# Max unpooling: the first load of the indices, issued as four transfers of every fourth partition instead of one

## The chip, the core and the metric

The kernel runs on one core of a Trainium2 chip. The metric is the device time of one execution in microseconds (us); lower is better. Most executions of one kernel lie within 0.3% of each other. In the profile the engines are VectorE (DVE), ScalarE (ACT), GpSimd (POOL) and SyncE (SP); a "q" after the name means the engine's own queue of waits and issues. Beside them, 16 DMA engines move data between the chip's memory and SBUF, the on-chip memory of 128 partitions.

## The reference

```python
x: (16, 64, 32, 32) float32;  indices: same shape, values 0 to 3;  kernel_size = 2
output = zeros((16, 64, 64, 64), float32)
output[b, c, 2*i + idx // 2, 2*j + idx % 2] = x[b, c, i, j]    # idx = indices[b, c, i, j]
```

Each input element goes to one of four places of a 2x2 block, the other three stay zero.

## The kernel before

The 1,024 images lie on 128 partitions, eight on each. The indices are 64-bit in memory, so eight images of them are 64 KiB for each partition, those of x 32 KiB, and the result 128 KiB. VectorE computes `(idx == p) * x` for each of the four places. Three loads are issued ahead of everything: three images of the indices, all of x, the other five images of the indices. Four stores, of two images each, follow as the images are done.

```python
FIRST = 3
cut = FIRST * 2 * N                         # N = 1024; 32-bit words, two for an index
program.first(nc.sync.dma_start(out=idx_t[:, :cut], in_=idx_v[:, :cut]).then_inc(idx_in[0], 16))
program.first(nc.sync.dma_start(out=x_t, in_=x_v).then_inc(x_in, 16))
program.first(nc.sync.dma_start(out=idx_t[:, cut:], in_=idx_v[:, cut:]).then_inc(idx_in[1], 16))

nc.vector.wait_ge(x_in, 16).then_inc(x_in, -16)
for t in range(T):                          # 8 images
    if t in (0, FIRST):
        half = int(t == FIRST)
        nc.vector.wait_ge(idx_in[half], 16).then_inc(idx_in[half], -16)
    ...                                     # cut: four scalar_tensor_tensor for one or two images
for g in range(NG):                         # 4 stores
    nc.sync.wait_ge(made, g + 1)
    nc.sync.dma_start(out=out_v[g], in_=out_t[g])
```

Of the kernel before, what the change touches and what calls it, by code (L numbers as in the profile page):

```python
# [1 line left out]

# [4 lines left out]

P = 128
F32 = mybir.dt.float32
I32 = mybir.dt.int32  # L10


class Program:




    def __init__(self, nc):
        self.nc = nc
        self.block = nc.main_func.blocks[0]  # L20
        self.kernel_block = nc.cur_bb.bb.name

    def __enter__(self):
        ins = self.block.instructions
        self.branches = [i for i in ins if "Branch" in type(i).__name__]
        n = len(ins) - len(self.branches)
        assert all("Branch" in type(ins[k]).__name__ for k in range(n, len(ins)))
        del ins[n:]
        self.nc.switch_bb(self.block.name, parent=None)
        self.symbolic = self.nc._always_lower_symbolic_ap  # L30
        self.nc._always_lower_symbolic_ap = False
        return self

    def first(self, made):
        ins = self.block.instructions
        assert ins[len(ins) - 1].name == made.ins.name
        moved = ins.pop()
        at = next(
            k
            for k, i in enumerate(ins)  # L40
            if i.engine == moved.engine and isinstance(i, mybir.InstDrain)
        )
        ins.insert(at, moved)

    def last(self, made):


        def move(nc):
            ins = self.block.instructions
            at = next(k for k, i in enumerate(ins) if i.name == made.ins.name)  # L50
            nc.main_func.blocks[-1].instructions.append(ins.pop(at))

        self.nc.at_finalize(move)

    def __exit__(self, kind, *_):
        self.nc._always_lower_symbolic_ap = self.symbolic
        if kind is None:
            for b in self.branches:
                self.block.instructions.append(b)
            self.nc.switch_bb(self.kernel_block, parent=None)  # L60


@with_exitstack
def kernel(
    ctx: ExitStack,
    tc: tile.TileContext,
    x: bass.AP,
    indices: bass.AP,
    kernel_size: bass.AP,
    out: bass.AP,  # L70
):
    nc = tc.nc
    assert kernel_size == 2

    B, C, H, W = x.shape
    n_img = B * C
    T = n_img // P
    assert T * P == n_img and C % T == 0

    G = 2  # L80
    NG = T // G
    FIRST = 3
    N = H * W
    x_v = x.rearrange("b (ch t) h w -> (b ch) (t h w)", t=T)
    idx_v = indices.rearrange("b (ch t) h w -> (b ch) (t h w)", t=T).bitcast(I32)
    out_v = out.rearrange("b (ch g t) oh ow -> g (b ch) (t oh ow)", g=NG, t=G)

    x_t = nc.alloc_sbuf_tensor("x_t", [P, T * N], F32).ap()
    idx_t = nc.alloc_sbuf_tensor("idx_t", [P, T * 2 * N], I32).ap()
    out_t = [  # L90
        nc.alloc_sbuf_tensor(f"out_t{g}", [P, G * 4 * N], F32).ap()
        for g in range(NG - 1)
    ]
    out_t.append(out_t[0])

    x_in = nc.alloc_semaphore("x_in")
    idx_in = [nc.alloc_semaphore(f"idx_in{g}") for g in range(2)]
    made = nc.alloc_semaphore("made")
    stored_0 = nc.alloc_semaphore("stored_0")
    stored = nc.alloc_semaphore("stored")  # L100

    x_c = x_t.rearrange("p (t i j) -> p t i j", t=T, j=W)
    idx_c = idx_t.rearrange("p (t i j two) -> p t i j two", t=T, j=W, two=2)[
        :, :, :, :, 0
    ]
    cut = FIRST * 2 * N

    with Program(nc) as program:
        program.first(
            nc.sync.dma_start(out=idx_t[:, :cut], in_=idx_v[:, :cut]).then_inc(  # L110
                idx_in[0], 16
            )
        )
        program.first(nc.sync.dma_start(out=x_t, in_=x_v).then_inc(x_in, 16))
        program.first(
            nc.sync.dma_start(out=idx_t[:, cut:], in_=idx_v[:, cut:]).then_inc(
                idx_in[1], 16
            )
        )

        nc.vector.wait_ge(x_in, 16).then_inc(x_in, -16)
        for t in range(T):
            g, k = t // G, t % G
            if t in (0, FIRST):
                half = int(t == FIRST)
                nc.vector.wait_ge(idx_in[half], 16).then_inc(idx_in[half], -16)  # L126

            if k == 1 and t != FIRST:
                continue
            n = 1 if k == 1 or t + 1 == FIRST else 2  # L130
            if g == NG - 1:
                nc.vector.wait_ge(stored_0, 16).then_inc(stored_0, -16)
            o_c = out_t[g].rearrange(
                "p (m i two j wo) -> p m i two j wo", m=G, two=2, wo=2, j=W
            )
            for pidx in range(4):
                op = nc.vector.scalar_tensor_tensor(  # L137
                    out=o_c[:, k : k + n, :, pidx // 2, :, pidx % 2],
                    in0=idx_c[:, t : t + n],
                    scalar=pidx,  # L140
                    in1=x_c[:, t : t + n],
                    op0=mybir.AluOpType.is_equal,
                    op1=mybir.AluOpType.mult,
                )
            if k + n == G:
                op.then_inc(made, 1)

        for g in range(NG):
            nc.sync.wait_ge(made, g + 1)
            nc.sync.dma_start(out=out_v[g], in_=out_t[g]).then_inc(  # L150
                stored if g else stored_0, 16
            )
        nc.sync.sem_inc(made, -NG)
        program.last(
            nc.sync.wait_ge(stored, 16 * (NG - 1)).then_inc(stored, -16 * (NG - 1))
        )


# [1 line left out]
_INS = ['x', 'indices', 'kernel_size']  # L160
_OUTS = [((16, 64, 64, 64), 'float32')]

_NUMBERS = {'kernel_size': 2}


# [26 lines left out]
```

## Time and profile before

| what | value |
|---|---|
| time, median | 71.49 us (71.4 to 71.7, 6 runs) |
| bytes | 12.58 MB read, 16.78 MB written |
| VectorE busy | 35.6 us |
| DMA engines busy | 97.4% of the span |

The span in the profile leaves out some 1.3 us of the device time. One thing has to be said ahead: the profile of before was taken on an execution of 71.79 us, 0.3 over the median. That becomes important when two profiles are compared.

The issues that open the program, and the start of VectorE, from the timeline (start, duration, engine, line, operation, names, count):

```profile
0.00 0.38 SPq L110 DMA_DIRECT2D idx_t<-in_indices_dram  x1
0.43 0.42 SPq L114 DMA_DIRECT2D x_t<-in_x_dram  x1
0.90 0.43 SPq L116 DMA_DIRECT2D idx_t<-in_indices_dram  x1
...
19.67 35.60 DVE L137 SCALAR_TENSOR_TENSOR out_t<-idx_t,x_t 128x2048 f32<-128x2048 int32 x20 [19.67 <-DVEq L126]
```

SyncE needs 0.38 to 0.43 us to issue a load and is done with all three at 1.33 us. The packet records in the trace, one for each row of each transfer, say when data began to move: at 1.00 us, 0.62 after the end of the first issue. The rest of the profile is read in the prediction.

### The profile page before, as it was taken

The numbers are of one execution on the slowest core, as the hardware profiler recorded it, in microseconds if no ns is written. First come the engines' busy times: TensorE is split into PE (matmuls) and PEld (weight loads), VectorE is DVE, ScalarE is ACT, GpSimd is POOL, SyncE is SP. The second block draws the span as 40 slices with busy tenths as digits, with TensorE's granted clock in tenths as the row PEclk, the third lists the DMA queues.
The fourth block names the chain that finished last, engine by engine and source line by source line (L and its number), as shares of the span: only waits on it lengthen the run. The fifth ranks groups of instructions, "written<-read, shape, count | busy, mean of one in ns | idle before, by whom it ended". The sixth has DMA issues, their size and how long they took to land.

```text
span 70.5 us, 72 instructions
## 1 busy us (share of the span) xinstructions
DVE 35.6 (51%) x20; POOL 0.2 (0%) x4
## 2 busy tenths in 40 slices
DVE  0000000000089999999999999999999300000000
POOL 1000000000000000000000000000000000000000
DMA  8799997979988999869898999989898989999891
GB/s 223 307 432 418 423 558 316 558 335 558 409 372 372 488 581 418 372 298 539 353 539 353 484 409 409 465 353 502 353 539 353 539 353 484 409 391 484 372 484 56
DMA packets 1008, 29.36 MB, mean 417 GB/s; under 512 B 112, under 2 KB 112, under 8 KB 112
## 3 DMA queue, kind: packets, MB, share of 16 engines
q1 hardware_dynamic: 1008, 29.36, 97.4%
HBM read 12.58 MB, written 16.78 MB: 417 GB/s over the span
## 4 chain that ended last, share of the span: by engine, by line
DVE 46%; DVEq 4%; issue 1%
DVE out_t L137 46%; DVEq L187 4%
## 5 line engine op out<-in xcount | busy, mean ns | idle before, releaser
L137 DVE SCALAR_TENSOR_TENSOR out_t<-idx_t,x_t 128x2048 f32<-128x2048 int32 (+1 forms) x20 | 35.6, 1860 | 19.7 <-DVEq L126 19.7
L173 POOL MEMSET const-bfloat16-1.0<- 128x1 bf16 x1 | 0.1, 103 | 0.0
L173 POOL MEMSET const-uint8-127<- 128x1 uint8 x1 | 0.1, 103 | 0.0
L173 POOL MEMSET const-float32-1.0<- 128x1 f32 x1 | 0.1, 100 | 0.0
L173 POOL MEMSET const-float32-0.0<- 128x1 f32 x1 | 0.1, 99 | 0.2 <-issue 0.2
## 6 DMA issues: line engine op xcount, KB each, us to landing
out_dram<-out_t SPq DMA_DIRECT2D x4, 4096.0 KB, 13.8
idx_t<-in_indices_dram SPq DMA_DIRECT2D x1, 5120.0 KB, 30.8
x_t<-in_x_dram SPq DMA_DIRECT2D x1, 4096.0 KB, 19.0
idx_t<-in_indices_dram SPq DMA_DIRECT2D x1, 3072.0 KB, 9.7
```

Of the source, the lines that this page charges most:

```text
L137: op = nc.vector.scalar_tensor_tensor(out=o_c[:, k : k + n, :, pidx // 2, :, pidx % 2], in0=idx_c[:, t : t + n], scalar=pidx, in1=x_c[:, t ...
L173: nc = _bacc.Bacc("TRN2", target_bir_lowering=False, num_devices=1)
L187: with _tile.TileContext(nc) as tc:
```

## The change

The first load becomes four transfers. Transfer o takes partitions o, o+4, ..., o+124, that is 32 rows spread over the whole of SBUF; such a transfer of every n-th partition is called a comb below. Bytes, row length and order of the three loads stay. The likely intent is to start with smaller transfers without giving up the reach over all partitions.

```diff
+    COMB = 4
 ...
-        program.first(
-            nc.sync.dma_start(out=idx_t[:, :cut], in_=idx_v[:, :cut]).then_inc(
-                idx_in[0], 16
+        for o in range(COMB):
+            rows = slice(o, None, COMB)
+            program.first(
+                nc.sync.dma_start(out=idx_t[rows, :cut], in_=idx_v[rows, :cut]).then_inc(
+                    idx_in[0], 16
+                )
             )
-        )
 ...
-                nc.vector.wait_ge(idx_in[half], 16).then_inc(idx_in[half], -16)
+                n_in = 16 if half else 16 * COMB
+                nc.vector.wait_ge(idx_in[half], n_in).then_inc(idx_in[half], -n_in)
```

## The prediction

> **What bounds the kernel now.** I read the busy tenths of the page first, then the DMA queue, then the stretches of the span one by one, then the chain that ended last. The page:
>
> ```profile
> span 70.5 us, 72 instructions
> ...
> DVE  0000000000089999999999999999999300000000
> ...
> DMA  8799997979988999869898999989898989999891
> ...
> q1 hardware_dynamic: 1008, 29.36, 97.4%
> HBM read 12.58 MB, written 16.78 MB: 417 GB/s over the span
> ```
>
> The reader is to see that VectorE works only in the middle (35.6 us of 70.5) and stops 15 us before the end, while the DMA row is full from the first slice to the last but one. The 16 DMA engines move packets for 97.4% of the span. The same in stretches that I cut at the borders of the transfers:
>
> ```profile
> 0.00:1.00 1.00, 0.00 (x0) 0.20 (x4) 1.00 0.00 0
> 1.00:2.00 1.00, 0.00 (x0) 0.00 (x0) 1.00 1.45 393
> 2.00:3.00 1.00, 0.00 (x0) 0.00 (x0) 1.00 0.89 369
> 3.00:5.00 2.00, 0.00 (x0) 0.00 (x0) 1.00 0.94 406
> 5.00:8.70 3.70, 0.00 (x0) 0.00 (x0) 1.00 0.99 425
> 8.70:18.40 9.70, 0.00 (x0) 0.00 (x0) 1.00 1.00 432
> 18.40:30.60 12.20, 10.93 (x6) 0.00 (x0) 1.00 1.00 432
> ```
>
> The last two columns are the DMA share and GB/s. Nothing moves in the first microsecond; the first load then climbs to 425 GB/s; from 8.7 us on it is flat at 432. (Shares above 1 only mean that a packet is counted whole at its start.)
>
> The packet records under this view give the arithmetic. There are 128 rows in each of seven transfers, 896 data packets, and 112 semaphore writes of 4 bytes. A row of 24,576 B takes 0.912 us, one of 32,768 B 1.213, one of 40,960 B 1.514; the next row on the same engine starts about 4 ns before the old one ends, so they cost 0.908, 1.210 and 1.511. Each engine has 8 rows of each transfer: 8 x (0.908 + 1.210 + 1.511 + 4 x 1.210) = 67.7 us. First packets start at 1.00 to 1.48 us and the last packet ends at 70.1. So no engine has more than about 2.4 us that is not steady transfer. On the engine that ends last I find them all: start 1.14, its first row 1.87 instead of 0.91 (0.96), one row of the second index load 0.25 too long. The first row is slow on all 16 engines (1.15 to 1.87), the second clearly so on three only, by at most 0.25, and no later row of this load.
>
> That VectorE does not matter is in the issues and the chain:
>
> ```profile
> SPq L150 <- DVE out_t L137: 52.5, 4, 26.9
> SPq L155 <- SPq L155: 14.1, 1, 14.1
> ```
>
> These are SyncE's waits. Stores are issued as images are done, the last at 55.3 us, but the third store's last bytes leave at 60.4 us, so the fourth waits in the rings for 4.3 us at least and up to 5 us: VectorE could be that much later at no cost. The page's chain (46% VectorE) does not see this queue; I don't follow it.
>
> [...] 32 rows still give 16 engines, two rows each, and 64 increments are the right count for four transfers. The trace agrees for 128 rows: eight rows for each of 16 engines, 16 semaphore writes for each transfer.
>
> [...] 24,576 B in 0.908 us is 27.1 GB/s on each engine, all 16 at once, without a row at half speed after the start. [...]
>
> [...] the three loads here queue behind each other without a gap.
>
> **The change, part by part.** Removed: one issue of 3,072 KB. Added: four of 768 KB with the same rows, row length and total bytes. An engine's share is still 8 rows of 24,576 B, 7.3 us.
>
> Issues: the three load issues took 0.38, 0.42 and 0.43 us of SyncE, one after the other from 0.00, 0.43 and 0.90. Three more delay the issue of x by 3 x 0.45 = 1.4 us, to about 1.8, and that of the second index load to about 2.3. The rings run dry only if an engine finishes two rows (1.8 us) before the next issue arrives (0.45 us later), so this is hidden. x is wanted at 8.8 us.
>
> Semaphore writes: three more for each engine. In the trace such a write takes 9 ns and the next row starts 6 ns after its start: 3 x 6 = 0.02 us. Nothing.
>
> Waits: VectorE waits for x (19.6 us) before it looks at the first index load; 64 increments instead of 16 cost it nothing.
>
> Start: the first packets still wait for the first issue, whose length does not seem to come from the number of rows (a store with rows of another size takes 0.34). If fewer rows meant sooner packets I could gain at most the spread of first starts, 0.48 us.
>
> Which rows an engine gets: this is the one part that can move the time. The transfer has partitions o, o+4, ..., o+124. Two ways to deal 32 rows to 16 engines:
> (a) [...] sum +0.0 to +0.1 us.
> (b) in consecutive pairs: [...] a row takes 1.82 instead of 0.91, eight rows 14.5 instead of 7.3: +7.3 us. [...] All later transfers and VectorE shift along; since the DMA stays the bound, all of it reaches the end.
>
> **The rivals.** First, the same (rival a): [...] It makes 71.5. Second, a gain at the start: shorter transfers, or other rows read at the same moment, could take away part of the slow first rows (0.25 to 0.96 us too long) or of the 0.8 us between the first and the last engine at the end. Against it: the first row of each engine is still its first, and byte counts are unchanged. All of it together is under 1.43 us, the 2% of 71.51; it makes 71.0. Third, issue starvation: every issue would have to cost over 1.8 us; measured 0.43. It makes nothing.
>
> **Range and chances.** The time has two humps: 71.2 to 71.7 (a), and about 75 to 78.8 (b), that is 71.5 plus 3.5 to 7.3. I hold (b) somewhat the likelier[...]. I choose a number in (b), with the discount for slipping: 71.5 + 5.0 = 76.5. The range has to span both. Slower 0.54, same 0.44, faster 0.02.
>
> **What would show it.** In (b): rows of the first load at 1.3 to 1.8 us throughout, the first 3.1 MB landing at about 13 to 16 us instead of 9.7 after issue, about 200 to 280 GB/s in the stretch 3 to 8.7 us, VectorE starting at about 25 instead of 19.67, and from x on everything as before (432 GB/s), only later. In (a): rows of 0.91 again from the third on, VectorE at 19.6 to 19.8, SyncE's six load issues over by 2.8 us. I would be wrong altogether if the rows after x changed their 1.21 us, if the DMA row showed a hole between the small transfers, or if the last store came to wait for VectorE.

## The result

The changed kernel takes 71.91 us (71.85 to 72.26, 6 runs) against 71.49: the same within 2%, and 0.69% slower (95% interval 0.41% to 0.96%). Here and below a ratio is the mean time of one kernel's fast runs over that of the other's of the same rounds, so it is not quite the ratio of the medians. The predicted 76.5 us did not come; the time fell into the lower of the prediction's two humps, a little above its upper edge.

The page of the changed kernel:

```profile
span 70.5 us, 75 instructions
...
DMA  7699989696988889966969696989979696969894
...
q1 hardware_dynamic: 1056, 29.36, 97.4%
HBM read 12.58 MB, written 16.78 MB: 416 GB/s over the span
```

There are 48 more packets, which are the semaphore writes of three more transfers (3 x 16). The DMA row is still full, and the first digit went from 8 to 7. The span is 70.5 us, the same as before. A reader who compares only these two pages would find no loss at all. But the first page is of an execution that took longer than usual (71.79 us; the six timed ones took 71.4 to 71.7). A second profile of the unchanged kernel, on one of 71.56 us, opens with

```profile
span 70.2 us, 72 instructions
```

so the pages agree with the loss that the timed runs show, and I compare with both profiles below.

The stretches of the changed kernel (the last two columns are DMA share and GB/s):

```profile
1.00:2.00 1.00, 0.00 (x0) 0.00 (x0) 1.00 1.47 369
2.00:3.00 1.00, 0.00 (x0) 0.00 (x0) 1.00 0.41 172
3.00:5.00 2.00, 0.00 (x0) 0.00 (x0) 1.00 1.13 479
5.00:8.70 3.70, 0.00 (x0) 0.00 (x0) 1.00 1.01 432
8.70:18.40 9.70, 0.00 (x0) 0.00 (x0) 1.00 1.01 437
```

A packet is counted whole at its start. With all 16 engines nearly in step this makes the second and third stretch look like a hole followed by a burst. It is none: first rows that began at 1.33 to 2.03 us last until about 3, and no engine pauses between two rows. From 5 us on the rate is 432 to 437 GB/s (before: 425 to 432). After the first rows nothing ran at half speed.

What did move is at the very beginning:

```profile
0.00 0.55 SPq L113 DMA_DIRECT2D idx_t<-in_indices_dram  x1
...
2.52 0.60 SPq L117 DMA_DIRECT2D x_t<-in_x_dram  x1
3.17 0.45 SPq L119 DMA_DIRECT2D idx_t<-in_indices_dram  x1
...
19.92 35.60 DVE L141 SCALAR_TENSOR_TENSOR out_t<-idx_t,x_t 128x2048 f32<-128x2048 int32 x20 [19.92 <-DVEq L130]
```

The first issue takes 0.55 us instead of 0.38, and the four together 2.48. VectorE starts at 19.92 us instead of 19.67, and does the same 35.6 us of work. A stepped issue is not the only thing that takes longer: the issue of x, whole as before, takes 0.60 us behind the four instead of 0.42; why is open.

The packet records do not name the DMA engine. But a packet starts some 4 ns before the one ahead of it on the same engine ends (6 ns after the start of a semaphore write), so they can be chained into 16 sequences. Each of the 16 has eight rows of the first load in both kernels; in the changed one they come in twos between semaphore writes in 14 of the 16, two rows of each of the four transfers. In these:

| packet records | before, 71.79 us | before, second profile, 71.56 us | changed, 71.85 us |
|---|---|---|---|
| very first packet starts (us) | 1.00 | 1.01 | 1.33 |
| first packet, mean of 16 engines | 1.16 | 1.23 | 1.52 |
| rows of the first load: median, and excess over it for each engine in all | 0.912, 0.57 | 0.912, 0.53 | 0.912, 0.66 |
| rows of x, mean start | 13.25 | 13.27 | 13.70 |
| last semaphore write: first, mean, last engine | 69.30, 69.57, 70.11 | 69.34, 69.55, 69.86 | 69.80, 69.96, 70.13 |

The excess is what the slow rows at the start, the ramp, cost beyond eight steady rows. The mean engine ends 0.39 to 0.42 us later, and it was already 0.43 to 0.45 late in the rows of x. So the whole loss is made in the first load. Against the second profile its terms are 0.29 (first packets), 0.13 (longer first rows) and 0.02 (semaphore writes), together 0.43. The last column also shows why the pages looked equal: the slowest engine in the first profile of before was 0.5 us behind the mean, in the changed kernel only 0.2.

### The profile page after: what moved, and what is told of

Read it like the earlier page. It is cut to its first block, busy times and chain, and to the rows that moved or that the text cites. A ratio compares the mean times of both kernels' runs of the same rounds, so it can differ in the third digit from the quotient of the medians.

```text
span 70.5 us, 75 instructions
## 1 busy us (share of the span) xinstructions
DVE 35.6 (50%) x20; POOL 0.2 (0%) x4
## 4 chain that ended last, share of the span: by engine, by line
DVE 46%; DVEq 4%; issue 1%
DVE out_t L141 46%; DVEq L191 4%
## 5 line engine op out<-in xcount | busy, mean ns | idle before, releaser
L141 DVE SCALAR_TENSOR_TENSOR out_t<-idx_t,x_t 128x2048 f32<-128x2048 int32 (+1 forms) x20 | 35.6, 1860 | 19.9 <-DVEq L130 19.9
```

The source lines that it names most:

```text
L141: op = nc.vector.scalar_tensor_tensor(out=o_c[:, k : k + n, :, pidx // 2, :, pidx % 2], in0=idx_c[:, t : t + n], scalar=pidx, in1=x_c[:, t ...
```

## The experiments

Two questions were open. Why were the rows not slow, although I thought it likelier that pairs of engines would slow each other down? (That they would was my assumption; no trace of the kernel before shows it.) And what made the start late? My theory after the result, called "late start" in the expectations: the four issues matter only through the first, which is longer and lets the first packets go 0.33 us later. The rival, "more transfers": it is the number of transfers. Each run below was timed beside the kernel before; ratios are to that. Issue times are from the timeline, packets from the packet records.

**e1_columns: four transfers of all partitions.**

```diff
-        for o in range(COMB):
-            rows = slice(o, None, COMB)
-            ... idx_t[rows, :cut] <- idx_v[rows, :cut]
+        for o in range(4):
+            cols = slice(o * cut // 4, (o + 1) * cut // 4)
+            ... idx_t[:, cols] <- idx_v[:, cols]
```

> First load as four transfers of all 128 partitions, a quarter of the columns each: as many issues and semaphore writes as the change, but no split over partitions. Late start (the theory: the issue of a 32-row transfer takes 0.55 us instead of 0.38 and its first packet starts 0.33 us later, and that is the whole loss): issues of 0.38 to 0.43 us, first packet at 1.00 us, time 71.4 to 71.6. More transfers (the rival: it is the number of transfers that costs): 71.8 to 72.0, as with the change.

Measured: 71.86 us, ratio 1.0055 (1.004 to 1.007). First issue 0.37 us, first packet at 1.01. The start was as my theory wanted, the time as the rival did. Taken alone this run speaks for the rival. But it changes something else: rows of 6,144 B. They follow each other every 0.231 us, so four cost 0.924 instead of 0.908; 8 x 0.016 is 0.13 us, and the semaphore writes are 0.02. The mean start of x is 0.19 to 0.20 late, so some 0.05 is lost in the ramp. That explains about half of the 0.36 us between the medians. The profiled execution, of 71.78 us, was only 0.22 over the second profile of before; the rest, which is not in it, I leave open. The run was a poor control, since it swapped one cost for another of like size.

**e3_comb_later: the comb where the engines are already busy.**

```diff
+        ... idx_t[:, :cut] <- idx_v[:, :cut]        # whole again
         ... x_t <- x_v
+        for o in range(4):
+            rows = slice(o, None, 4)
+            ... idx_t[rows, cut:] <- idx_v[rows, cut:]
```

> The first load whole, the second load of the indices as four transfers of every fourth partition: the same transfers where the engines are already busy. Late start: 71.4 to 71.6, nothing lost, since the long issues lie beside the first load. More transfers: 71.8 to 72.0. [...]

Measured: 71.62 us, ratio 1.0014 (1.0002 to 1.0026). Rows of the second load 1.514 us as before. The comb issues took 0.54 to 0.59 us each here too, but beside a running load. At the edge of the expected range: a tenth of a microsecond may be left, not four.

**e4_lead_image: a short whole transfer ahead of the comb.**

```diff
+        ... idx_t[:, :2 * N] <- idx_v[:, :2 * N]    # image 0, 128 rows of 8,192 B
         for o in range(4):
-            ... idx_t[rows, :cut] <- idx_v[rows, :cut]
+            ... idx_t[rows, 2 * N:cut] <- idx_v[rows, 2 * N:cut]
```

> Image 0 as one transfer of 128 rows first, images 1 and 2 as four transfers of every fourth partition behind it. Late start: first packets at 1.00 us again and 71.4 to 71.6. More transfers: 71.9 or more. A row of 8,192 B takes 0.30 us, eight of them 2.4, enough to cover the first comb issue of 0.6 us.

Measured: 71.73 us, ratio 1.0023 (1.0009 to 1.0037); first packet at 1.02. This has one transfer more than the change, five for the first load, and loses a third (by the ratios) to a half (by the medians) of what the change loses. That is against the rival, and 0.1 over what my theory expected. When x starts, e4 is only 0.05 us behind the second profile of before, which is about what its shorter rows cost (0.306 + 0.608 instead of 0.908 us, eight times); the change is 0.43 behind there. What e4 lost later is not explained.

**e7_x_then_comb and e8_x_then_whole: the clean pair.** The same transfers as in the changed kernel and in the kernel before, but x goes first in both.

```diff
+        ... x_t <- x_v                              # first, in e7 and in e8
         for o in range(COMB):                       # e7; in e8 one whole transfer here
             ...
-        ... x_t <- x_v
```

> The change with x (128 whole rows of 32,768 B) issued first and the four comb transfers behind it; nothing else differs. Late start: first packet at 1.00 to 1.02 us again, the four long issues hidden beside x, and the time within 0.1 us of the same order without a comb (e8). If the comb's rows or its 48 semaphore writes cost by themselves: 0.3 to 0.4 us over e8.

> The control of e7: the kernel before with x issued first, the first index load whole behind it. Both theories: 71.4 to 71.6, since VectorE waits for both loads anyway.

Measured: e7 71.71 us (1.0022, 1.0003 to 1.0041), e8 71.77 us (1.0028, 1.0012 to 1.0044). With x ahead, the comb costs nothing that these runs can see: e7's mean is 0.04 us under e8's, give or take 0.17 (95%), so a cost of 0.1 could hide here, one of 0.4 could not. In e7 the timeline opens with

```profile
0.00 0.37 SPq L110 DMA_DIRECT2D x_t<-in_x_dram  x1
0.43 0.53 SPq L113 DMA_DIRECT2D idx_t<-in_indices_dram  x1
```

The long issue is there, in second place, and the first packet starts at 0.99 us. So the comb costs time only where it opens the program, which is what the late start says; the number of transfers as the cause falls. (I expected 71.4 to 71.6 for e8; x first is itself some 0.2 slower. In its profile the rows of x lose 0.62 us for each engine to the ramp, where the first index load lost 0.53 to 0.57 in the two profiles of before.)

**e2_blocks32 and e5_comb8: does it matter which partitions a transfer covers?** Four blocks of 32 neighbouring partitions, and eight combs of 16 rows. For each I held two outcomes possible: rows of about twice the time (1.6 to 1.9 us, 76 to 80 us in all), or rows of 0.91 us and about 72.

```diff
-            rows = slice(o, None, 4)
+            rows = slice(32 * o, 32 * (o + 1))      # e2, four transfers
+            rows = slice(o, None, 8)                # e5, eight transfers, semaphore count 128
```

> First load as four transfers of 32 neighbouring partitions, no stride. [...] rows of 1.6 to 1.82 us instead of 0.91 through the first load, time 76 to 79. [...] 71.9, as with the change, and then the change says nothing on how rows are dealt. Issue: if the stride makes it longer, 0.38 us here; if the 32 rows do, 0.55.

> Eight transfers of every eighth partition, 16 rows each. [...] rows of about 1.8 to 1.9 us again and 77 to 80 us. If e2 was slow because its partitions are neighbours [...]: rows of 0.91 and about 72 us. Issue, if the step makes it long: 0.55 us or more each.

Measured: e2 79.08 us (1.106, 1.1042 to 1.1078), e5 79.27 us (1.1077, 1.1057 to 1.1097). The stretches of e2:

```profile
3.00:5.00 2.00, 0.00 (x0) 0.00 (x0) 1.00 1.02 209
5.00:8.70 3.70, 0.00 (x0) 0.00 (x0) 1.00 0.97 206
8.70:18.40 9.70, 0.00 (x0) 0.00 (x0) 1.00 0.95 245
```

and those of e5:

```profile
3.00:5.00 2.00, 0.00 (x0) 0.00 (x0) 1.00 1.02 209
5.00:8.70 3.70, 0.00 (x0) 0.00 (x0) 1.00 0.99 206
```

The DMA share is 1 all the time (0.95 to 1.02 in these stretches), the engines are "busy", and the rate is half. A busy share alone hides this; one has to read GB/s beside it. Rows take 1.91 us (e2) and 1.90 (e5) at the median, all through the first load, and do not slip apart although first packets start 0.6 us (e2) and 1.0 us (e5) apart. e5 has a partition step like the change and still halves. So it is not neighbourhood alone. What else e2 and e5 have in common was not shown. Two rivals are left in e5: its rows also lie 512 KiB apart in memory (256 in the change), and a transfer has 16 of them instead of 32; no run separates these from the partitions covered. For e2 the runs e9 and e10 below do separate the two sides; for e5 the equal row time, 1.90 against 1.91 us, is the argument.

The issues tell a second thing. The first issue of e2:

```profile
0.00 0.39 SPq L112 DMA_DIRECT2D idx_t<-in_indices_dram  x1
```

and of e5:

```profile
0.00 0.59 SPq L112 DMA_DIRECT2D idx_t<-in_indices_dram  x1
```

32 rows without a step cost 0.39 us, and the first packet starts at 1.02. With a step the first packet of e5 starts at 1.36. For the first issue of a program it is the step, not the smaller number of rows.

**e6_comb2: two combs of 64 rows.**

```diff
-            rows = slice(o, None, 4)
+            rows = slice(o, None, 2)                # two transfers, semaphore count 32
```

> Two transfers of every second partition, 64 rows each[...]. [...] rows of 0.91 us. If in consecutive fours: [...] rows of 1.6 us or more and 76 to 79 us. Late start: a step of any size makes the issue 0.55 us and the first packet 1.33 us, and the time is 71.8 to 72.0, as with four; if the number of transfers costs, half of the loss: 71.7.

Measured: 71.93 us, ratio 1.0051 (1.0033 to 1.0068), rows 0.91, issues of 0.55 and 0.58 us, first packet at 1.33. Half the transfers, and the loss is not halved: the late start again. And transfers of 64 rows, too, ran at the full rate.

**e9_sbuf_step and e10_dram_step: which step?** Was e2 slow because of the partitions it writes or because of the order of its rows in memory, and which of the two sides makes the start late? Wrong results on purpose; the rows land on other partitions.

```diff
+            step, block = slice(o, None, 4), slice(32 * o, 32 * (o + 1))
+            ... idx_t[step, :cut] <- idx_v[block, :cut]     # e9
+            ... idx_t[block, :cut] <- idx_v[step, :cut]     # e10
```

> Wrong result on purpose: each of the four transfers reads 32 neighbouring rows of memory and writes every fourth partition, so only the destination has a step. If the step in the partitions makes the late start: issue 0.55 us, first packet at 1.33, 71.8 to 72.0. If the step in memory does: issue 0.38 to 0.40, first packet at 1.00 to 1.02, 71.5. Rows of 0.91 us either way[...]; rows of 1.9 would say that the order in memory[...] slowed e2.

> Wrong result on purpose, the mirror of e9: each transfer reads every fourth row of memory and writes 32 neighbouring partitions. [...] rows of 1.9 us and 79 us here too; if the order in memory did: rows of 0.91 and about 72. Issue and first packet: the reverse of e9 (0.39 and 1.02 if the partitions' step makes the late start, 0.55 and 1.33 if the memory's does; both long if either step is enough).

Measured: e9 72.01 us (1.0082, 1.0065 to 1.01), e10 79.09 us (1.1061, 1.1046 to 1.1077); both results wrong, as meant. First issue of e9:

```profile
0.00 0.55 SPq L112 DMA_DIRECT2D idx_t<-in_indices_dram  x1
```

and of e10:

```profile
0.00 0.39 SPq L112 DMA_DIRECT2D idx_t<-in_indices_dram  x1
```

The same stretch of the first load in e9,

```profile
5.00:8.70 3.70, 0.00 (x0) 0.00 (x0) 1.00 1.04 445
```

and in e10:

```profile
5.00:8.70 3.70, 0.00 (x0) 0.00 (x0) 1.00 0.99 206
```

First packets at 1.33 and 1.02, rows of 0.91 and 1.91. Both questions get the same answer: the partitions' side decides. A step there makes the start late; a block there halves the rate. The order in memory does neither, for the step of four rows that was tried.

**e11_x_from_act: an attempt at something better than both.** The kernel before, with x issued by ScalarE.

```diff
-        program.first(nc.sync.dma_start(out=x_t, in_=x_v).then_inc(x_in, 16))
+        program.first(nc.scalar.dma_start(out=x_t, in_=x_v).then_inc(x_in, 16))
```

> An attempt at a version better than both: the kernel before with x issued from ScalarE's queue, so that two queues start the 16 engines. If the walk of one issue over the engines sets the spread of first packets (1.00 to 1.48 us) and the queues take different engines first, the mean first packet comes up to 0.15 us sooner: 71.3 to 71.4. If both walk in the same order, or x's rows only interleave: 71.5, same.

Measured: 71.71 us, ratio 1.0028 (1.0016 to 1.0041), so a little slower. First packets start at a mean of 1.27 us, no sooner (1.16 and 1.23 before); what sets their spread was not shown. The last semaphore writes of all engines fall within 0.17 us (69.78 to 69.95), the tightest of all runs, but their mean is 0.3 later than in the kernel before.

**e0_before_again: a second profile of the kernel before.**

```diff
(no edit)
```

> The kernel before once more, for a second profile: the one at hand is of a run of 71.79 us, 0.3 over its usual time. I expect a span of 70.1 to 70.2, first packet at 1.00 us, and the last engine at 69.7 to 69.8 instead of 70.1.

Measured (a single run, for its profile): 71.56 us, span 70.2, first packet at 1.01, last engine at 69.86. As expected but for a tenth in the last number; its column in the table above is from this run.

## Why the prediction was wrong

**The bound.** Right. DMA engines set the time: in the changed kernel, in e2 and in e5 what is lost at the start is found at the end, be it 0.4 us or 7.6. The slack of VectorE is put about 1 us too high: the wait of the fourth store is counted from its issue, but in the profile a first issue and the way to its first packet take 1.0 us, so some 3.3 us of the 4.3 are free. Nothing hung on it.

**Issues, semaphore writes, waits.** Right in kind. The issues were dearer than the assumed 0.45 us (2.48 us for four), but no engine paused between two rows (each starts some 4 ns before the one ahead ends), and e7 shows that the four together are hidden when something else goes first. SyncE's issues were over at 3.62 us, not 2.8.

**Start: the step that failed in the accounting.** I wrote that the length of the first issue "does not seem to come from the number of rows". That is true (e2: 0.39 us for 32 rows), but by luck: the store that I gave as evidence has 128 rows too, and I looked for no other cause. The step in the partitions makes it 0.55, and the first packet goes 0.33 later. This was read as a possible gain of up to 0.48 us, and was a loss: it is most of what the change costs (0.29 of the 0.43 us; longer first rows are 0.13), and it put the time 0.2 above the hump that I gave for rows at the full rate. Why the packet is later by twice what the issue is longer stays open.

**Which rows an engine gets: the step that failed in the verdict.** I held the deal in consecutive pairs (b) likelier than one that keeps the rate (a), and chose 71.5 + 5.0. The term measured zero: rows of 0.912 us. That pairs would slow each other was my assumption, and which engine gets which row was not shown: no record names the engine of a packet. What the runs show is that the partitions of a transfer can halve its rate. Blocks of 32 neighbours did, by +7.58 us (79.08 - 71.50) in e2, where my estimate was +7.3, for rows of twice the measured 0.91; they took 1.91 where I had 1.82. Every eighth partition took 1.90 (e5), while every fourth (0.912) and every second (0.91, e6) ran at the full rate. The reason was not shown.

**The discount for slipping apart.** Not tested; the 5.0 instead of 7.3 was my estimate. In e2 and e5 rows stayed at 1.9 us although the engines did not start together (first packets 0.6 and 1.0 us apart), so nothing slipped apart there. Whether the deal that I feared would have cost 5 us or the full 7.6 stays open.

**The weighing.** What spoke for pairs was only that I had seen nothing that tied another deal to 32 rows. The absence of evidence is weak evidence, and I let it outweigh what the code showed: a stride of four spreads each transfer over the whole of SBUF, which suggests an author who counts on that reach. The lower hump was right but for the late start; the size of the upper one is close to what rows at half the rate cost in e2 (79.08 us, the hump's edge was 78.8). The number was put on the wrong one.

## What to carry to other kernels

In a kernel bound by its transfers, it can matter which partitions each part of a split load covers: parts of every second or fourth partition kept the full rate here (rows of 0.91 us), blocks of 32 neighbours or every eighth partition halved it (rows of 1.91 and 1.90 us, 206 GB/s), and the busy share of the DMA engines showed none of that. No split here was faster than the one transfer. Don't put a transfer with a partition step first in a program: here its issue was 0.17 us longer and its first packet 0.33 us later, and at the start nothing hides that. And before two profiles are compared, look at which execution each was taken on; here equal spans hid a loss of 0.4 us.
